# A hybrid decoder block on one core: GpSimd subtracts 1,024 columns in four instructions of 256

## The chip, the cores and the metric

The kernel runs on one core of a Trainium2 chip. The metric is the device time of one execution in microseconds, as the median of several runs. The engines are called PE (TensorE's matmuls; PEld are its weight loads), DVE (VectorE), ACT (ScalarE), POOL (GpSimd) and SP (SyncE, which here issues the loads).

## What is computed

One layer of a decoder block on x of 256 tokens by 1,024 channels, in f32. The reference, cut to what matters:

```python
mod = (c @ w_ada + b_ada)                       # 6 x 1024: shifts, scales, gates
h = rms_norm(x, norm_mix) * (1 + sc_m) + sh_m
q_a, kv_a, gl_a, qkv_b, a_b, b_b, z_b, merge = split(h @ w_in)
y_a = nsa_attention(q_a, kv_a, gl_a, ...)       # 16 heads, three branches
y_b = gated_deltanet(qkv_b, a_b, b_b, z_b, ...) # 8 heads, chunked delta rule
mixed = g_a * (y_a @ w_proj_nsa) + g_b * (y_b @ w_proj_gdn)
x = x + gt_m * (mixed @ w_out)
h = rms_norm(x, norm_ffn) * (1 + sc_f) + sh_f
u = causal_depthwise_conv(h @ ffn_up, ffn_conv) + ffn_conv_b
x = x + gt_f * ((silu(u_gate) * u_val) @ ffn_down)
return rms_norm(x, norm_final)
```

## The kernel before

Nearly all the work is matrix products with weights that are read from HBM once, some 118 MB. Each product is done to more than the precision of one pass: a weight w is split into hi, w rounded to the matmul's input type, and lo = w - hi, the activations likewise, and each block of the product is three matmuls: hi times hi, hi times the activation's lo, and lo times the activation's hi (`lin`, lines 255 to 271).

A weight comes in pieces of 128 partitions by 1,024 columns (512 KB). `rawload` (229) asks SP for the load into a ring of five raw buffers, tag `wraw`. `split` (234) then makes hi with a copy on ACT (243) and lo with a subtraction on POOL or DVE (244). The raw buffer is free again when both have read it. hi lies in one of five buffers and lo in one of four, and they are free when TensorE has read them. The down-projection's pieces have buffers of their own (dhi, dlo). Who subtracts is counted out: every second piece goes to POOL in the opening, all of them from line 353 on, and three of five from line 755 on (`pool_share`). In `lin` a piece of 1,024 columns is four blocks of 256, one for each k of 128 input channels, and the matmuls of a block read its 256 columns of hi and lo; one piece feeds 2 x 4 x 3 = 24 matmuls.

The same five raw buffers carry the columns of w_ada (48 pieces, tag `wada`). They take no part in matmuls: DVE multiplies a piece with a broadcast c and sums it up (`adasum`, line 214), which gives 128 entries of mod. In the opening (lines 344 to 349) each of the eight k needs two such sums, then the scaled activation `mt` (298), its hi on ACT (306) and its lo on DVE (307), and two weight pieces of the projection `wko`, one subtracted by DVE and one by POOL.

The order of the opening up to line 341 is written by hand. From there on a planner, which keeps its own times for every instruction, orders the instructions of each engine's queue; the loads on SP stand in one queue, in which a load that waits for its buffer holds up those behind it. `recent` remembers the last instruction on an engine, and some later instructions are put behind it (lines 758, 1069 to 1075).

POOL has other work besides: the low half of the queries (line 884), 64 partitions by 256 columns, one of the weightings of the attention's probabilities (922), a mask (552) and the scaling of keys (524). The lines of DVE that the text names are 465 to 468, small steps of the gates with 16 or 32 columns, and 214 and 244. In the feed-forward part DVE does the taps of the convolution (1114) with one operand in PSUM.

Of the kernel before, what the change touches and what calls it, by code (L numbers as in the profile page):

```python
# [11 lines left out]
F32 = mybir.dt.float32  # L12
# [4 lines left out]
ALU = mybir.AluOpType  # L17
# [5 lines left out]
D = 1024  # L23
# [78 lines left out]
def build(tc, a, probe=None):  # L102
    nc = tc.nc
    V, S, G, TE = nc.vector, nc.scalar, nc.gpsimd, nc.tensor
    with ExitStack() as ctx:
# [17 lines left out]
        def tl(name, tag, shape=None, dt=F32):  # L123
            n, w = TAGS[tag]
            return wk.tile(list(shape or (P, w)), dt, name=name, tag=tag, bufs=n)
# [100 lines left out]
        recent = {}  # L226
# [7 lines left out]
        def split(w, down=False):  # L234
            if down:
                hi, lo = tl("dhi", "dh", dt=F32R), tl("dlo", "dh", dt=F32R)
            else:
                hi = wp.tile([P, D], F32R, name="whi", tag="whi", bufs=5)
                lo = wp.tile([P, D], F32R, name="wlo", tag="wlo", bufs=4)
            cnt[0] += 1  # L240
            n, m = pool_share[0]
            e = G if cnt[0] * n // m != (cnt[0] - 1) * n // m else V
            recent[S] = S.copy(hi, w).ins  # L243
            recent[e] = e.tensor_tensor(lo, w, hi.bitcast(F32), op=ALU.subtract).ins  # L244
            return hi, lo

        def loadw(src, down=False):

            return [split(rawload(src[i]), down) for i in range(src.shape[0])]
# [87 lines left out]
        t = scaled(0)  # L337
        shifted(0, t, V)
        ko(0, 0, *split(wko[0]))
        ko(0, 1, *split(wko[1]))  # L340
        start.close()

# [93 lines left out]
        w = wp.tile([P, D], F32, name="wraw", tag="wraw", bufs=NRAW)  # L436
        nc.sync.dma_start(out=w[:, :512], in_=a["wg"])
        w = w[:, :512].rearrange("p (k c) -> p k c", k=KB)
# [100 lines left out]
        for h in range(NH):  # L539
            for c in range(2):  # L540
# [5 lines left out]
                e = tl("e", "tg")  # L546
# [8 lines left out]
                            op=ALU.add, negate=True)  # L555
# [55 lines left out]
        n = range(2)  # L611
# [523 lines left out]
        for f in range(NF):  # L1135
# [8 lines left out]
            t, w = o  # L1144
# [31 lines left out]
        for k in range(KB):  # L1176
            (G if k in POOLK else V).tensor_tensor(x2b[k], x2b[k], r, op=ALU.mult)
            if k in OUTS:
                lo = OUTS[k]
# [66 lines left out]
```

## Time and profile before

| what | us |
|---|---|
| runs | 655.29, 654.51, 653.84 |
| median | 654.51 |
| profiled execution, device time | 651.43 |
| its span, first to last instruction | 649.4 |
| busy: PE, DVE, ACT, POOL | 583.3, 512.1, 381.5, 342.1 |

The profile is of one execution. A row of a group gives the number of instructions, their busy time in all, the mean of one in ns, and the idle time of the engine just ahead of them with what ended it. An instruction that stands still after its start, for whatever reason, counts as busy. The chain is found from the last instruction back, at each step to what released it or to the instruction before it on its engine. Matmuls are pipelined, so that their durations overlap. Spans on POOL are rough.

### The profile page before, as it was taken

To read this page: it belongs to the slowest core of one execution; us is meant where nothing else is said; L and a number is where in the kernel's file an instruction comes from. 1 tells how busy PE (TensorE), PEld (TensorE's weight loads), DVE (VectorE), ACT (ScalarE), POOL (GpSimd) and SP (SyncE) were. 2 spreads that over 40 slices of the span, in tenths; PEclk is the share of its full clock that TensorE was granted. 3 is DMA by queue.
4 is the path that set the end of the run, shared out by engine and by line. 5 is a ranking of instruction groups with operands and counts; after the bars stand their busy time and mean duration, and the time that the engine had idled before them with its cause. 6 is when DMAs were issued, how large, how long until landed. Compare 5 with 4: busy or idle time off the path is not lost.

```text
span 649.4 us, 13709 instructions
## 1 busy us (share of the span) xinstructions
PE 583.3 (90%) x5128; PEld 550.4 (85%) x5128; DVE 512.1 (79%) x1206; ACT 381.5 (59%) x858; POOL 342.1 (53%) x239
## 2 busy tenths in 40 slices
PE   7888999899988888999898998698599999999794
PEld 4787998788988886999776998698599999989793
DVE  5999869789999998697967789697966576766845
ACT  4335988645565686596776633376765545435554
POOL 3324897735666877365631435265474545435531
PEclk9999999999998899899999999799699999999998
DMA  7789665344675744234414456864557456566401
GB/s 293 272 288 338 207 210 191 110 153 133 225 257 203 245 147 147 83 98 132 147 49 164 136 183 207 318 224 134 184 180 246 168 195 229 195 223 230 165 1 65
DMA packets 35364, 119.73 MB, mean 184 GB/s; under 512 B 4961, under 2 KB 5729, under 8 KB 35298
## 3 DMA queue, kind: packets, MB, share of 16 engines
q1 hardware_dynamic: 35298, 118.86, 53.6%
q8 instruction: 40, 0.66, 0.4%
q14 instruction: 26, 0.21, 0.1%
HBM read 117.66 MB, written 1.18 MB: 183 GB/s over the span
## 4 chain that ended last, share of the span: by engine, by line
PE 40%; DVE 35%; DMA 10%; ACT 7%; issue 6%; POOL 1%; SPq 0%; DVEq 0%; ACTq 0%; POOLq 0%
PE lin L266 8%; PE lin L268 8%; PE lin L269 8%; DMA wada<-in_ada 8%; DVE wlo L244 7%; DVE wada L214 6%; DVE pp L922 2%; PE dn L1132 2%; PE dn L1131 2%; PE dn L1130 2%; PE y L968 1%; ACT whi L243 1%; DVE cacc L398 1%; DMA wraw<-in_down 1%; DVE tb L577 1%
## 5 line engine op out<-in xcount | busy, mean ns | idle before, releaser
L244 POOL TENSOR_TENSOR wlo<-wraw,whi 128x1024 fp32r<-128x1024 f32 x90 | 228.8, 2551 | 165.3 <-ACT whi L243 97.4
L243 ACT CAST whi<-wraw 128x1024 fp32r<-128x1024 f32 x144 | 150.0, 1048 | 67.9 <-PE lin L268 20.9
L266 PE MATMUL lin<-hh,whi 128*128 128x256 f32 x384 | 111.2, 290 | 1.1 <-DVE cacc L398 0.7
L268 PE MATMUL lin<-hl,whi 128*128 128x256 f32 x384 | 110.7, 289 | 0.0
L269 PE MATMUL lin<-hh,wlo 128*128 128x256 f32 x384 | 110.5, 289 | 0.0
L214 DVE CUSTOM_DVE_ANT_0 wada<-wada,cb,col 128x1024 f32<-128x1024 f32 x48 | 86.1, 1795 | 22.2 <-DMA wada<-in_ada 22.0
L266 PE MATMUL lin<-fh,whi 128*128 128x256 f32 x304 | 85.6, 282 | 8.8 <-DVE up L1148 8.8
L269 PE MATMUL lin<-fh,wlo 128*128 128x256 f32 x304 | 86.0, 283 | 5.7 <-DVE wlo L244 3.9
L244 DVE TENSOR_TENSOR wlo<-wraw,whi 128x1024 fp32r<-128x1024 f32 x54 | 88.1, 1632 | 2.8 <-ACT whi L243 2.2
L268 PE MATMUL lin<-fl,whi 128*128 128x256 f32 x304 | 85.5, 281 | 0.0
L266 PEld LDWEIGHTS lin<-hh,whi 128*128 128x128 f32 x384 | 74.1, 193 | 2.0 <-ACT whi L243 0.9
L269 PEld LDWEIGHTS lin<-hh,wlo 128*128 128x128 f32 x384 | 74.1, 193 | 0.8 <-issue 0.3
L268 PEld LDWEIGHTS lin<-hl,whi 128*128 128x128 f32 x384 | 74.0, 193 | 0.6
L266 PEld LDWEIGHTS lin<-fh,whi 128*128 128x128 f32 x304 | 58.3, 192 | 9.0 <-ACT fh L1103 9.0
L269 PEld LDWEIGHTS lin<-fh,wlo 128*128 128x128 f32 x304 | 58.3, 192 | 7.0 <-DVE wlo L244 5.0
L244 POOL TENSOR_TENSOR dlo<-wraw,dhi 128x1024 fp32r<-128x1024 f32 x14 | 37.4, 2676 | 49.8 <-ACT dhi L243 48.4
L268 PEld LDWEIGHTS lin<-fl,whi 128*128 128x128 f32 x304 | 58.4, 192 | 0.0
L1132 PE MATMUL dn<-ah,dlo 128*128 128x256 f32 x176 | 48.8, 277 | 0.6 <-POOL dlo L244 0.6
L1131 PE MATMUL dn<-al,dhi 128*128 128x256 f32 x176 | 48.6, 276 | 0.0
L1130 PE MATMUL dn<-ah,dhi 128*128 128x256 f32 x176 | 48.6, 276 | 0.0
L915 ACT ACTIVATE pp<-pp,misc 128x128 f32<-128x128 f32 x64 | 28.4, 446 | 13.5 <-DVE misc L907 13.4
L1132 PEld LDWEIGHTS dn<-ah,dlo 128*128 128x128 f32 x176 | 33.1, 188 | 1.0 <-POOL dlo L244 1.0
(410 smaller groups left out, 1597.7 us busy)
## 6 DMA issues: line engine op xcount, KB each, us to landing
wraw<-in_win SPq DMA_DIRECT2D x52, 512.0 KB, 3.6
wada<-in_ada SPq DMA_DIRECT2D x48, 512.0 KB, 3.9
wraw<-in_up SPq DMA_DIRECT2D x44, 512.0 KB, 4.2
wraw<-in_down SPq DMA_DIRECT2D x22, 512.0 KB, 3.8
wraw<-in_wko SPq DMA_DIRECT2D x16, 512.0 KB, 5.2
wraw<-in_pn SPq DMA_DIRECT2D x8, 512.0 KB, 3.5
wraw<-in_pg SPq DMA_DIRECT2D x8, 512.0 KB, 3.5
wraw<-in_wo SPq DMA_DIRECT2D x8, 512.0 KB, 3.9
```

Source lines behind the costliest of these rows:

```text
L214: V.tensor_tensor_reduce(w, w, cb, 1.0, cl("bada", m), ALU.mult, ALU.add, mod[:, m:m + 1])
L243: recent[S] = S.copy(hi, w).ins
L244: recent[e] = e.tensor_tensor(lo, w, hi.bitcast(F32), op=ALU.subtract).ins
L266: TE.matmul(o[:, b], hi[:, j, cs], hh[k], start=k == 0 and b == 0, stop=False, skip_group_check=True)
L268: TE.matmul(o[:, b], hi[:, j, cs], hl[k], start=False, stop=False, skip_group_check=True)
L269: TE.matmul(o[:, b], lo[:, j, cs], hh[k], start=False, stop=k == KB - 1 and b == blocks - 1, skip_group_check=True)
L398: V.scalar_tensor_tensor(acc[:, sft:], src[:, :T - sft], col[:, w0 + 3 - sft:w0 + 4 - sft], acc[:, sft:], op0=ALU.mult, op1=ALU.add)
L915: S.activation(pv, pv, AF.Exp, bias=mx[:, 1 + w, t, r:r + 1], accum_out=sm[:, 1 + w, t, r:r + 1])
L922: (G if 2 * w + t in POOLP else V).tensor_scalar(pv, pv, wt[:, 1 + w, t, r:r + 1], None, op0=ALU.mult)
L1130: TE.matmul(o, hi[:, cs], ah, start=f == 0 and b % 2 == 0, stop=False, skip_group_check=True)
L1131: TE.matmul(o, hi[:, cs], al, start=False, stop=False, skip_group_check=True)
L1132: TE.matmul(o, lo[:, cs], ah, start=False, stop=f == NF - 1 and b % 2 == 1, skip_group_check=True)
```

## The change

Where POOL does a subtraction, it does so in four instructions of 256 columns each, one behind the other; where DVE does, the instruction stays one of 1,024. `recent` then holds the fourth.

```diff
             recent[S] = S.copy(hi, w).ins
-            recent[e] = e.tensor_tensor(lo, w, hi.bitcast(F32), op=ALU.subtract).ins
+
+            n = 4 if e is G else 1
+            for i in range(n):
+                c = slice(D // n * i, D // n * (i + 1))
+                recent[e] = e.tensor_tensor(lo[:, c], w[:, c], hi[:, c].bitcast(F32), op=ALU.subtract).ins
             return hi, lo
```

## Rows read from the trace of the kernel before

**Rows 1.** The page's busy times: engine, us, share of the span, instructions.
```profile
PE 583.3 (90%) x5128; PEld 550.4 (85%) x5128; DVE 512.1 (79%) x1206; ACT 381.5 (59%) x858; POOL 342.1 (53%) x239
```

**Rows 2.** The page's chain that ended last, shares of the span by engine.
```profile
PE 40%; DVE 35%; DMA 10%; ACT 7%; issue 6%; POOL 1%; SPq 0%; DVEq 0%; ACTq 0%; POOLq 0%
```

**Rows 3.** Line 244 alone: ns of one, min/median/max; first and last start in us.
```profile
L244 POOL TENSOR_TENSOR wlo<-wraw,whi x90: 2345/2406/3484, 14.2 to 604.9; 128x1024 fp32r<-128x1024 f32 x90
L244 DVE TENSOR_TENSOR wlo<-wraw,whi x54: 1191/1219/3403, 14.5 to 609.5; 128x1024 fp32r<-128x1024 f32 x54
L244 POOL TENSOR_TENSOR dlo<-wraw,dhi x14: 2402/2409/3397, 461.9 to 628.6; 128x1024 fp32r<-128x1024 f32 x14
```

**Rows 4.** Groups of DVE by form, and line 214 alone (min/median/max).
```profile
L244 DVE TENSOR_TENSOR wlo<-wraw,whi 128x1024 fp32r<-128x1024 f32 x54 | 88.1, 1632 | 2.8 <-ACT whi L243 2.2 <-PE lin L269 0.3 <-ACT zt L751 0.2
L214 DVE CUSTOM_DVE_ANT_0 wada<-wada,cb,col 128x1024 f32<-128x1024 f32 x48 | 86.1, 1795 | 22.2 <-DMA wada<-in_ada 22.0
...
L214 DVE CUSTOM_DVE_ANT_0 wada<-wada,cb,col x48: 1235/1285/3448, 9.2 to 585.4; 128x1024 f32<-128x1024 f32 x48
```

**Rows 5.** Timeline of DVE, 50 to 56 us: start, us, instruction, idle before.
```profile
50.78 3.25 DVE L214 CUSTOM_DVE_ANT_0 wada<-wada,cb,col 128x1024 f32<-128x1024 f32 x1 [0.31 <-DMA wada<-in_ada]
```

**Rows 6.** Timeline of POOL, 50 to 56 us.
```profile
50.55 2.40 POOL L244 TENSOR_TENSOR wlo<-wraw,whi 128x1024 fp32r<-128x1024 f32 x1 [4.58 <-ACT whi L243]
```

**Rows 7.** Timeline of DVE, 95 to 103 us.
```profile
95.57 1.55 DVE L465 TENSOR_TENSOR misc<-misc,col 128x16 f32<-128x16 f32 x1
97.04 2.42 DVE L466 TENSOR_SCALAR misc<-misc 128x16 f32<-128x16 f32 x1
```

**Rows 8.** Timeline of POOL, 92 to 103 us (merged), and the last of the four alone.
```profile
89.98 9.45 POOL L244 TENSOR_TENSOR wlo<-wraw,whi 128x1024 fp32r<-128x1024 f32 x4
...
97.05 2.37 POOL L244 TENSOR_TENSOR wlo<-wraw,whi 128x1024 fp32r<-128x1024 f32 x1
```

**Rows 9.** Timeline of DVE and of POOL, 221 to 233 us.
```profile
221.69 1.33 DVE L214 CUSTOM_DVE_ANT_0 wada<-wada,cb,col 128x1024 f32<-128x1024 f32 x1
...
222.02 3.27 POOL L244 TENSOR_TENSOR wlo<-wraw,whi 128x1024 fp32r<-128x1024 f32 x1
```

**Rows 10.** The chain in order of time: start, us, what.
```profile
14.55 3.41 DVE wlo L244
...
47.09 3.67 DMA wada<-in_ada
...
54.07 3.84 DMA wada<-in_ada
...
609.46 2.21 DVE wlo L244
...
626.27 5.73 POOL dlo L244 x2
```

**Rows 11.** Lines 884 and 552 alone on POOL: ns, min/median/max.
```profile
L884 POOL TENSOR_TENSOR qq<-qT,qq x32: 716/733/1695, 84.2 to 324.7; 64x256 fp32r<-64x256 f32 x32
...
L552 POOL TENSOR_TENSOR um<-U,cst x8: 625/628/1606, 130.7 to 167.3; 128x256 f32<-128x256 f32 x8
```

**Rows 12.** Windows: us, busy PE, PEld, DVE, ACT, POOL; then line 244's DVE, POOL.
```profile
72.00:135.00 63.00, 59.37 (x486) 56.50 (x485) 50.30 (x126) 49.60 (x148) 49.22 (x34) 1.00 0.52 170
465.00:600.00 135.00, 133.25 (x1151) 132.59 (x1150) 89.04 (x136) 71.03 (x111) 68.87 (x27) 0.99 0.60 206
...
72.00:135.00 63.00, 2.54 (x2) 39.95 (x17) 1.00 0.52 170
```

**Rows 13.** SP's own waits: line, waited for whom, us in total, times, longest.
```profile
SPq L231 <- POOL wlo L244: 107.8, 45, 5.3
...
SPq L210 <- POOL wlo L244: 28.8, 7, 7.5
```

## The prediction, made before the changed kernel was run

> **What bounds the kernel now.** I began with the busy times. TensorE's matmuls fill 90% of the span, VectorE (DVE) 79%, GpSimd (POOL) 53% [rows 1]. The chain that ended last names another culprit beside TensorE: 40% of the span lies on PE, 35% on DVE, 10% on transfers, 1% on POOL [rows 2]. So POOL, the engine that the change touches, sets the end almost nowhere by itself; the reader is to ask what it does to DVE.
>
> The spread of one instruction answers that. Line L244 on DVE takes 1.219 us at the median and 3.403 at most; on POOL 2.406 and 3.484 [rows 3]. The groups of DVE have means far above the clean time: L244 1632 ns against 1219, the adaLN sum of L214 1795 against its median of 1285 [rows 4]. That is 54 x 0.41 = 22 us and 48 x 0.51 = 24 us of waiting inside the instructions. The timeline shows why. The adaLN sum that starts at 50.78 meets a POOL subtraction which began at 50.55 and runs 2.40; it ends at 54.03, 1.08 us after POOL [rows 5, 6]. A DVE instruction that works within SBUF stands still until the whole POOL instruction is over. It is no matter of length: L466, one operand of 16 columns, took 2.42 us beside a POOL subtraction of 2.37 [rows 7, 8]. It goes the other way too: a POOL subtraction that starts while the sum at 221.69 runs takes 3.27 us [rows 9].
>
> How much of it lies on the chain? From the piece at 14.55 (3.41 us) to the one at 609.46 (2.21), 23 of its pieces are L244 or L214 stretched beyond 1.22 and 1.29 us; their excess sums to 33 us [rows 10]. Short instructions such as L465 and L466 (1.55 and 2.42 us for 16 columns) [rows 7] add some 20 more by the same count, an estimate. So about **53 us of 649** is DVE on the chain, waiting for POOL.
>
> **The change, part by part.** All subtractions keep their engine; 90 + 14 = 104 POOL instructions of 1,024 columns [rows 3] become 416 of 256.
>
> *Price of a piece.* The trace holds no such piece. The nearest rows are L884, the same operation over 256 columns on 64 partitions, 0.733 us at the median, and L552, 256 columns on 128 partitions with a multiply, 0.628 [rows 11]. POOL's neighbours in a row overlap by some 0.03 us: four subtractions from 89.98 took 9.45 us, 2.36 each [rows 8]. Four pieces then last 4 x 0.628 - 3 x 0.03 = 2.42 to 4 x 0.733 - 0.09 = 2.84 us, against 2.41. I take 2.84, the row of the same operation: **+0.43 us each, 45 us of POOL in all**, 342 to 387 of 649. The lower end is +0.01, 1 us in all.
>
> *Where POOL's extra lies.* Mostly beside idle time. The critical stretch is 72 to 135 us, where every subtraction goes to POOL: 49.2 of 63 us busy, PE 59.4 [rows 12]. One POOL subtraction feeds 24 matmuls, and TensorE, at 1151 matmuls in 135 us [rows 12], passes 24 in 2.8 us: POOL at 2.84 just keeps up, but its lead shrinks. Seventeen subtractions there cost 7 us, more than half of 13.8 us of POOL idle. If that cover is gone TensorE waits for all 7 or 8 us. Against it stands that the first piece is there after 0.73 us where the whole came after 2.41, and matmuls that read one block of the weight can begin on it. I take +2 us, bounds 0 and +8. At the end two subtractions in a row (626.27, 5.73 us) stand on the chain [rows 10]; the last piece comes 0.9 later, but TensorE starts on earlier pieces: 0, bounds -2 and +1.
>
> *What DVE gets back.* An instruction that waits now waits for a piece, not for the rest of 2.40 us. Since the sum at 50.78 ended 1.08 us after POOL and needs 1.285 alone, 0.2 of a wait is covered; a piece costs at most 0.73 - 0.20 = 0.53. But POOL is back in the queue after every piece, so a second DVE instruction of this kind can meet the second piece: four waits of 0.53 are 2.1, and one whole wait today is 2.40 - 0.20 = 2.2. Where DVE runs such instructions without a pause, **the total stays as it is**. That is the case at 14 to 72 us. Its round runs from one load of a column block of `ada` to the next, 47.09 to 54.07 [rows 10]: the load takes 3.67, then the sum at 50.78 takes 3.25 and frees the buffer for the next load. That sum would end 1.7 us earlier, and the load behind it would go out earlier; but the second sum, mt and wlo then meet the other three pieces. The round's 6.98 us hold 0.31 in which DVE waits for the load and 3.25 - 1.29 = 1.96 in which it waits for POOL [rows 5]; the 4.71 that are left, plus 2.12, are 6.83. Some 12 of the 53 us lie in this stretch, and I book 0, bounds -1 (six rounds of 0.15) and +8 (the third rival's).
>
> Elsewhere 53 - 12 = 41 us remain. The 23 pieces waited 1.4 us on average; two waits of about 0.35 in place of it halve them: **-20 us** on this chain. What is late next: TensorE, full at 465 to 600 us (133.25 of 135) [rows 12], and the ring of raw buffers with transfers of 3.7 us and more [rows 10]. I give half to them: **-10**, bounds 0 and -20.
>
> *Waits that the change adds.* None is written, but SP sends the next load when POOL's last piece has released its raw buffer; SP stood on POOL 45 + 7 times, 107.8 + 28.8 us, with all later loads queued behind [rows 13]. ACT's casts wait for those loads. This price is the third rival's.
>
> *Order of the queues.* Outside the opening the planner orders the work by its own times of each instruction, and four short ones are other entries than one long. No row prices that; I bound it by one ring transfer of 3.8 us [rows 10] either way, taken as 0.
>
> Sum: -10 + 2 = **-8 us**. The profiled execution took 651.43 us (span 649.4), so 643.4 there; it lies 3.1 under the median of 654.51, and against that the time is **646.5**.
>
> **A rule that speaks against it.** The Trainium skill (SBUF — State Buffer, section Who interferes with whom) says that the shared port pair is held for a whole instruction, and that issue order decides which side blocks. [Rows 9] agree that POOL can be the blocked side. By that rule each piece is a new turn in which POOL may be the one to wait, and the time is the third rival's 662 us; by the idle time of POOL in [rows 1] it is 646.5.
>
> **Rivals.** *Larger gain.* Nearly all 41 us leave the chain and half of that shows: -20 + 2 = -18, 636.5 us. For it: PE waits stand behind DVE's. Against: PE 90% busy. Chance 0.13.
>
> *Hidden.* DVE's waits shrink, but the next chain, PE with its buffers, is as long; within 1.3 us of 654.5. Chance 0.10.
>
> *POOL hands the buffers back late (slower).* Where DVE is dense, each piece waits for a 1.2 us instruction, and a subtraction takes 4 x (0.53 + 1.2) = 6.9 us instead of 2.41 to 3.48. A raw buffer is free 0.4 to 3.4 us later, say 1.5; over 52 waits of SP that is 78 us of later issue, and with 10% of the span's chain on transfers, +8: 662 us. It decides once more than half of the pieces wait for DVE. For it: [rows 13]. Against: POOL idles 47%. Chance 0.22.
>
> *The pieces do not let DVE in.* Then the edit does not do what it says: 53 us of waits grow by 0.43/2.40, 9.5 us, half of it shown, +5: 659 us. Against it: L465 (95.57, 1.55) ended at 97.12, although the next POOL subtraction had already begun at 97.05 [rows 7, 8]; so DVE got its turn between neighbours. The Trainium skill (GPSIMD Engine Reference, section Instruction dispatch) says that a core starts the next instruction when its own share is done, without waiting for the other cores; by that rule no instant need be free between pieces. Chance 0.05.
>
> **How the numbers follow.** My forecast has 0.47, with a range of its own of 640 to 652. A further 0.03 for a planner's order that costs time. Faster 0.47 + 0.13 = 0.60, no difference (within 0.2%, which is about what a measurement of this kernel can tell) 0.10, slower 0.22 + 0.05 + 0.03 = 0.30. The range reaches from below the larger gain, 634, to the ring's 662.
>
> **What would show it.** Right: L244 on POOL 416 times near 0.73 us; L214's mean nearer 1.4 than 1.8 us and no DVE instruction of 16 columns above 0.8; DVE's share of the chain well under 35%. Wrong in the step of halving: L214 and L244 on DVE still average over 1.6 us. Wrong by the ring: SP's wait for POOL far above 137 us, TensorE waiting for POOL's wlo. Wrong by price: pieces above 0.8 us when nothing holds them, POOL above 70% of the span.

## The result and the profile after

The changed kernel took **633.35 us** (median of four runs, 628.62 to 635.48) against 654.17 of the kernel before (four runs, 650.24 to 655.29): a ratio of 0.9682, 95% interval 0.9614 to 0.975, 20.8 us less. The forecast was 646.5 with a range of 634 to 662: the sign was right, the time lies just below the range, and the gain was more than twice the forecast one. The profiled execution after took 628.62 us with a span of 626.8; it is the fastest of the four, 4.7 below their median, so between the two profiles 22.6 us of span are to be explained. The lines of the code have moved by four (244 is now 248). In three of the later kernels one run each took over 1.5% longer than the fastest of the same kernel; it is left out of their times.

The page's busy times and the shares of the chain, which answer to [rows 1, 2]:

```profile
PE 579.2 (92%) x5128; PEld 546.3 (87%) x5128; DVE 468.0 (75%) x1206; ACT 382.5 (61%) x858; POOL 431.5 (69%) x551
...
PE 53%; DVE 17%; DMA 10%; ACT 7%; POOL 7%; issue 3%; SPq 1%; DVEq 0%; ACTq 0%; POOLq 0%
```

DVE lost 44 us of busy time with the same 1,206 instructions, POOL gained 89. On the chain DVE went from 35% of 649 us (227) to 17% of 627 (107); PE went from 40% to 53% and POOL from 1% to 7%. Span minus PE's busy time is 66.1 us before and 47.6 after: 18.5 of the 22.6 us are time in which TensorE had nothing to do, 4.1 are its matmuls themselves.

Line 248 alone (ns, min/median/max), the two DVE groups with their means, and line 214 alone, which answer to [rows 3, 4]:

```profile
L248 POOL TENSOR_TENSOR wlo<-wraw,whi x360: 718/738/1792, 14.5 to 588.4; 128x256 fp32r<-128x256 f32 x180
L248 POOL TENSOR_TENSOR dlo<-wraw,dhi x56: 723/740/1797, 446.6 to 607.7; 128x256 fp32r<-128x256 f32 x56
L248 DVE TENSOR_TENSOR wlo<-wraw,whi x54: 1206/1240/1765, 14.6 to 585.7; 128x1024 fp32r<-128x1024 f32 x54
...
L248 DVE TENSOR_TENSOR wlo<-wraw,whi 128x1024 fp32r<-128x1024 f32 x54 | 74.4, 1377 | 4.7 <-ACT whi L243 3.9 <-PE lin L273 0.7
L214 DVE CUSTOM_DVE_ANT_0 wada<-wada,cb,col 128x1024 f32<-128x1024 f32 x48 | 70.4, 1470 | 29.6 <-DMA wada<-in_ada 29.4
...
L214 DVE CUSTOM_DVE_ANT_0 wada<-wada,cb,col x48: 1270/1384/1871, 9.7 to 562.7; 128x1024 f32<-128x1024 f32 x48
```

The longest DVE subtraction for `wlo` is 1.77 us where it was 3.40; the means fell from 1632 to 1377 and from 1795 to 1470 ns. The starts on POOL tell where the time was gained, as far as the new order leaves the same work in the same place. Beside those of `dlo` above, the low halves of the queries (line 884, now 888) answer to [rows 11]:

```profile
L888 POOL TENSOR_TENSOR qq<-qT,qq x32: 717/734/1753, 85.6 to 318.4; 64x256 fp32r<-64x256 f32 x32
```

The first low half of the queries starts at 85.6 us where it was 84.2, so the opening gained nothing that shows there; the last starts 6 us earlier (318.4 against 324.7), the first `dlo` 15 us (446.6 against 461.9) and the last 21 us (607.7 against 628.6). Behind the opening the gain is spread over the kernel.

What was one wait is now several short ones. The timelines of DVE and of POOL at 50 us [rows 5, 6], then of DVE at 94 us [rows 7]:

```profile
50.16 1.81 DVE L214 CUSTOM_DVE_ANT_0 wada<-wada,cb,col 128x1024 f32<-128x1024 f32 x1 [0.83 <-DMA wada<-in_ada]
...
52.16 1.49 DVE L214 CUSTOM_DVE_ANT_0 wada<-wada,cb,col 128x1024 f32<-128x1024 f32 x1
...
50.16 4.97 POOL L248 TENSOR_TENSOR wlo<-wraw,whi 128x256 fp32r<-128x256 f32 x4 [2.30 <-ACT whi L243]
...
94.61 0.48 DVE L469 TENSOR_TENSOR misc<-misc,col 128x16 f32<-128x16 f32 x1
95.01 0.78 DVE L470 TENSOR_SCALAR misc<-misc 128x16 f32<-128x16 f32 x1
```

The sum that took 3.25 us takes 1.81, and the 16-column step that took 2.42 takes 0.78. POOL pays: its four pieces between DVE's instructions took 4.97 us. By themselves they cost what was forecast, as POOL's timeline at 577 us shows, with POOL's groups (the two groups stood at 228.8 and 37.4 us before):

```profile
577.63 2.83 POOL L248 TENSOR_TENSOR dlo<-wraw,dhi 128x256 fp32r<-128x256 f32 x4 [2.59 <-ACT dhi L243]
...
L248 POOL TENSOR_TENSOR wlo<-wraw,whi 128x256 fp32r<-128x256 f32 x360 | 307.5, 887 | 105.0 <-ACT whi L243 51.7 <-PE lin L273 22.5 <-issue 20.1
L248 POOL TENSOR_TENSOR dlo<-wraw,dhi 128x256 fp32r<-128x256 f32 x56 | 46.7, 868 | 32.8 <-ACT dhi L243 23.0 <-issue 9.8
```

Four pieces in 2.83 us, where 2.84 had been taken. The groups sum to 354.2 us, 88 more than 266.2: 45 are the price of the pieces, and the other 43 are longer waits for DVE, an estimate from these sums.

The windows of [rows 12], SP's waits of [rows 13] and TensorE's waits for POOL's low halves:

```profile
72.00:135.00 63.00, 60.43 (x495) 56.96 (x494) 48.19 (x132) 52.07 (x152) 59.03 (x85) 1.00 0.52 164
465.00:600.00 135.00, 133.25 (x1161) 132.45 (x1160) 83.02 (x140) 73.37 (x114) 93.25 (x108) 1.00 0.63 207
...
SPq L231 <- POOL wlo L248: 123.0, 61, 5.5
SPq L210 <- POOL wlo L248: 53.9, 15, 8.9
...
PE ko L318 <- POOL wlo L248: 2.3, 5, 0.9
PE lin L273 <- POOL wlo L248: 1.6, 2, 1.1
```

At 72 to 135 us POOL is now busy 59.0 of 63, with 4.0 idle where 13.8 were; yet TensorE passes 495 matmuls there instead of 486. SP stands on POOL for 177 us instead of 137, and TensorE waits 3.9 us in all for these pieces, where it waited 3.3 for POOL's whole subtractions.

### The profile page after: what moved, and what is told of

It is laid out like the page before. It is cut to its first block, busy times and chain, and to the rows that moved or that the text cites. A ratio compares the mean times of both kernels' runs of the same rounds, so it can differ in the third digit from the quotient of the medians.

```text
span 626.8 us, 14062 instructions
## 1 busy us (share of the span) xinstructions
PE 579.2 (92%) x5128; PEld 546.3 (87%) x5128; DVE 468.0 (75%) x1206; ACT 382.5 (61%) x858; POOL 431.5 (69%) x551
## 4 chain that ended last, share of the span: by engine, by line
PE 53%; DVE 17%; DMA 10%; ACT 7%; POOL 7%; issue 3%; SPq 1%; DVEq 0%; ACTq 0%; POOLq 0%
PE lin L270 11%; PE lin L273 11%; PE lin L272 11%; DMA wada<-in_ada 6%; POOL wlo L248 5%; PE dn L1135 3%; PE dn L1136 3%; PE dn L1134 3%; DVE wada L214 3%; ACT whi L243 2%; DVE wlo L248 2%; DMA wraw<-in_wko 2%; DVE pp L926 2%; PE y L972 1%; DMA wraw<-in_win 1%
## 5 line engine op out<-in xcount | busy, mean ns | idle before, releaser
L248 POOL TENSOR_TENSOR wlo<-wraw,whi 128x256 fp32r<-128x256 f32 x360 | 307.5, 887 | 105.0 <-ACT whi L243 51.7
L270 PE MATMUL lin<-hh,whi 128*128 128x256 f32 x384 | 109.7, 286 | 1.1 <-DVE cacc L402 1.1
L272 PE MATMUL lin<-hl,whi 128*128 128x256 f32 x384 | 109.1, 285 | 0.0
L270 PE MATMUL lin<-fh,whi 128*128 128x256 f32 x304 | 85.6, 282 | 8.7 <-DVE fl L1108 8.7
L214 DVE CUSTOM_DVE_ANT_0 wada<-wada,cb,col 128x1024 f32<-128x1024 f32 x48 | 70.4, 1470 | 29.6 <-DMA wada<-in_ada 29.4
L248 DVE TENSOR_TENSOR wlo<-wraw,whi 128x1024 fp32r<-128x1024 f32 x54 | 74.4, 1377 | 4.7 <-ACT whi L243 3.9
L273 PEld LDWEIGHTS lin<-hh,wlo 128*128 128x128 f32 x384 | 72.8, 190 | 1.7 <-POOL wlo L248 1.0
L248 POOL TENSOR_TENSOR dlo<-wraw,dhi 128x256 fp32r<-128x256 f32 x56 | 46.7, 868 | 32.8 <-ACT dhi L243 23.0
L318 PE MATMUL ko<-hh,wlo 128*128 128x256 f32 x128 | 32.7, 289 | 2.8 <-POOL wlo L248 2.3
```

The lines of the kernel that those rows point to most:

```text
L214: V.tensor_tensor_reduce(w, w, cb, 1.0, cl("bada", m), ALU.mult, ALU.add, mod[:, m:m + 1])
L248: recent[e] = e.tensor_tensor(lo[:, c], w[:, c], hi[:, c].bitcast(F32), op=ALU.subtract).ins
L270: TE.matmul(o[:, b], hi[:, j, cs], hh[k], start=k == 0 and b == 0, stop=False, skip_group_check=True)
L272: TE.matmul(o[:, b], hi[:, j, cs], hl[k], start=False, stop=False, skip_group_check=True)
L273: TE.matmul(o[:, b], lo[:, j, cs], hh[k], start=False, stop=k == KB - 1 and b == blocks - 1, skip_group_check=True)
L318: TE.matmul(kob[4 * w + b // 2][:, b % 2], m[:, b * P:b * P + P], h[k], start=k == 0 and i == 0 and b % 2 == 0, stop=k == KB - 1 and i == ...
```

## The experiments

Three things can carry the gain. **Hold**: a POOL instruction holds up DVE for a quarter of the time. **Order**: the planner sees four entries instead of one and orders all queues anew. **Early word**: each piece tells TensorE that it is there, so that the first matmuls need not wait for the fourth. The runs take them apart. All kernels compute the whole reference; each ratio is to the kernel before, run on the same chip in between, with its 95% interval. Where the order is to be kept, the list of instructions is rewritten after the planner is done.

### The hold alone: the old order, pieces told at the fourth

```diff
+def in_pieces(n):
...
+            for j in range(n):
+                s = mybir.SyncInfo(on_wait=list(i.sync_info.on_wait) if j == 0 else [],
+                                   on_update=list(i.sync_info.on_update) if j == n - 1 else [])
+                out.append(mybir.InstTensorTensor(
...
+    regroup(nc, in_pieces(4))
```

> Every queue as before; only, after planning, each POOL subtraction is four instructions of 256 columns, and whoever waits for it waits for the fourth. Theory A (DVE waits for a quarter of a subtraction): 633 to 640 us, the line of the subtraction and the adaLN sum on DVE near 1.4 us on average. Theory B (the planner's new order of the queues makes the gain): 652 to 660. Theory C (TensorE begins on the first quarter): no gain either, 652 or more, since nothing is told before the fourth.

Measured: 645.33 us (643.53 to 648.27), ratio 0.9875 (0.9837 to 0.9913). Its busy times, chain, DVE's sums, and TensorE's waits for the low halves (lines as before the change):

```profile
PE 582.5 (91%) x5128; PEld 552.6 (86%) x5128; DVE 469.7 (73%) x1206; ACT 382.0 (60%) x858; POOL 425.9 (66%) x551
PE 44%; DVE 15%; DMA 15%; POOL 13%; ACT 7%; issue 5%; SPq 1%; DVEq 0%; POOLq 0%; ACTq 0%
...
L214 DVE CUSTOM_DVE_ANT_0 wada<-wada,cb,col 128x1024 f32<-128x1024 f32 x48 | 69.4, 1448 | 38.4 <-DMA wada<-in_ada 35.8
...
PE ko L314 <- POOL wlo L244: 8.0, 6, 2.8
PE lin L269 <- POOL wlo L244: 7.4, 4, 3.5
```

DVE gets back just what it does in the changed kernel (469.7 us busy against 468.0, the sums at 1448 ns against 1470), but the time falls by 8 us only (653.1 for the kernel before in these runs); all three ranges that had been expected miss it. DVE's share of the chain is 15% where it was 35%, and POOL (13%, was 1%) and transfers (15%, were 10%) have grown. The chain in order of time shows how, in the feed-forward part:

```profile
506.38 2.14 POOL dlo L244 x3
508.52 0.97 POOL wlo L244 x2
509.87 5.21 POOL wlo L244 x6
515.09 4.42 DMA wraw<-in_down
...
598.60 3.79 POOL wlo L244 x4
```

A load waits for a raw buffer that POOL's pieces hand back late, which is the forecast's third rival. In the changed kernel the chain has a single entry of pieces between 435 and 615 us (585.42, 3.77 us); the others lie before that.

### The order alone: the new order, each four joined to one instruction

103 of the 104 groups are joined; of one the pieces don't stand side by side.

```diff
+            take = joined if merge else (lambda ap: ap)
...
+            if merge and not last:
+                continue
...
+    regroup(nc, told_late(True))
```

> The queues as the planner orders them for the four short instructions, but the four joined to one of 1,024 columns where they stand next to one another. A: no gain, 650 to 660, DVE's means back above 1.6 us. B: 633 to 640. C: no gain.

Measured: 648.86 us (648.22 to 649.72), ratio 0.9926 (0.9898 to 0.9953). The chain and DVE's sums:

```profile
DVE 36%; PE 23%; DMA 21%; ACT 11%; issue 6%; POOL 2%; SPq 0%; DVEq 0%; ACTq 0%; POOLq 0%
...
L214 DVE CUSTOM_DVE_ANT_0 wada<-wada,cb,col 128x1024 f32<-128x1024 f32 x48 | 89.8, 1872 | 31.1 <-DMA wada<-in_ada 30.8
```

DVE's waits are back, and with them most of the time; 648.86 lies just below the 650 to 660 of the first theory. The order by itself is worth some 4 us against the same 653.1; hold and order, each alone, make 8 + 4 = 12 of 21.

### The early word taken away, in the new order

```diff
-    regroup(nc, told_late(True))
+    regroup(nc, told_late(False))
```

> The changed kernel with its four short instructions, but the first three tell nobody that they are done; the waits of all others end with the fourth. A: at most 3 us above the changed kernel, 633 to 637. B: the same. C: most of the gain is gone, 645 to 655.

Measured: 640.95 us (634.28 to 643.28), ratio 0.9824 (0.979 to 0.9859). About 8 us more than the changed kernel, with runs 9 us apart, and between the ranges that had been expected. The chain, and TensorE's waits for the low halves, in its fastest run:

```profile
PE 49%; DVE 16%; POOL 12%; ACT 9%; DMA 8%; issue 5%; SPq 1%; DVEq 0%; POOLq 0%; ACTq 0%
...
PE ko L318 <- POOL wlo L248: 10.4, 7, 2.6
PE lin L273 <- POOL wlo L248: 4.0, 4, 1.5
```

14.4 us of waiting where the changed kernel has 3.9. So the early word counts here: it takes back what the late end of the pieces costs TensorE. Told late, POOL has 12% of the chain in the new order too, where the changed kernel has 7%.

Hold and order add up: pieces told late gain 7.8 us in the old order (653.1 to 645.33) and 7.9 in the new one (648.86 to 640.95), and both together make some 12. The other 8 or 9 us come with the early word.

### The early word added, in the old order; and the changed kernel again

Each piece now raises POOL's semaphore, and a matmul waits for the piece of its own block.

```diff
+                    piece = a.offset % D // (D // n) + 1
+                    if piece > g[1]:
...
+                        waits.append(wait(g[2], g[0] + piece if piece < n else g[3]))
...
+    regroup(nc, told_early(4))
```

> Order of the queues as before, four pieces, and now each piece tells TensorE of its own end; matmuls of a block of 256 columns wait for their block's piece alone. If the three parts add up (shorter holds of DVE -8, waits for a quarter -7, planner's order -4): 636 to 640. If the early word helps only in the planner's new order: 643 to 647, as with the wait for the fourth.

> The changed kernel once more, beside the others of this call. All theories: 631 to 636, about 7 us under the 641 that it took with the waits ending at the fourth piece.

Measured: 645.93 us (640.96 to 650.04), ratio 0.988 (0.9842 to 0.9918), and beside it the changed kernel at 631.64 (630.23 to 633.34), ratio 0.9663 (0.9636 to 0.9689). In the old order the early word gains nothing. Its busy times, chain and TensorE's waits (lines one further down), and windows (us, then PE, PEld, DVE, ACT and POOL busy, the granted clock, DMA share, GB/s):

```profile
PE 589.4 (92%) x5128; PEld 557.6 (87%) x5128; DVE 470.2 (73%) x1206; ACT 381.9 (59%) x858; POOL 428.6 (67%) x551
PE 45%; DVE 15%; POOL 14%; DMA 14%; issue 6%; ACT 6%; SPq 0%; DVEq 0%; POOLq 0%; ACTq 0%
...
PE lin L270 <- POOL wlo L245: 3.0, 4, 1.1
PE ko L315 <- POOL wlo L245: 1.6, 3, 0.9
...
550.00:559.00 9.00, 9.00 (x82) 9.00 (x81) 5.81 (x11) 3.53 (x6) 7.90 (x9) 1.00 0.79 264
574.00:580.00 6.00, 6.00 (x32) 6.00 (x32) 3.73 (x6) 2.68 (x5) 2.07 (x3) 0.54 0.84 268
```

TensorE's waits for POOL did fall, from 15.4 to 4.6 us, and its idle time (spans of 641.7 and 643.6, minus busy) from 59.2 to 54.2. But the same 5,128 matmuls took 6.9 us longer: at 574 to 580 us, behind a stretch with gaps, the granted clock was 0.54, near the lower level of 1.2 GHz, and 32 matmuls passed in 6 us where 82 pass in 9 at full clock. And POOL is on the chain as before (14%).

With the early word in both, **the order is worth 14.3 us**: 645.93 against 631.64; told late, it was worth 4.4 (645.33 against 640.95). Between the two profiles with the early word lie 13.7 us of span (643.6 and 629.9): TensorE's idle time makes 6.7 of them (54.2 against 47.5) and slower matmuls 7.0 (589.4 us busy against 582.4, at mean granted clocks of 0.953 and 0.969).

### Half of the early word

The changed kernel with the first three pieces silent in the first 41 of the 104 groups, or in the others.

```diff
+        whole &= set(names[:41])
```

> The changed kernel, in which the first 41 of 104 subtractions (those of the first 205 us) tell only at the fourth piece and the others at each. If the early word pays where POOL works without a pause and TensorE follows close behind it (opening and 72 to 135 us): most of the loss of the late word, 638 to 642. If it pays in the rest: 631 to 634.

```diff
+        whole &= set(names[41:])
```

> The complement: the first 41 subtractions tell at each piece, the other 63 at the fourth. By the first theory 631 to 635; by the second 637 to 642.

Measured: 633.61 us (628.36 to 636.81), ratio 0.9683 (0.9645 to 0.9721), and 634.24 (631.77 to 637.56), ratio 0.9714 (0.9685 to 0.9743). Neither half loses more than some 3 us, and both intervals overlap that of the changed kernel, so neither theory came out. The 8 or 9 us of the whole don't split into places; this stayed open.

### How many pieces

In the old order, two pieces told at the second, and two pieces each told; with the planner two, three (256, 256, 512) and eight.

```diff
+    regroup(nc, in_pieces(2))
```

> Order of before, each POOL subtraction two instructions of 512 columns. A: a DVE instruction waits at most 1.0 instead of 2.2 us, so a good half of the gain of four pieces: 640 to 647. B and C: none, 652 to 656.

```diff
+    regroup(nc, told_early(2))
```

> The same with two pieces of 512 columns that each tell TensorE. Two pieces cost POOL less and took 643 with the late word. If the early word is worth its share for the first half: 637 to 641. If POOL's extra time is what limits four pieces, this one is level with four early pieces or below it.

```diff
-            n = 4 if e is G else 1
+            n = 2 if e is G else 1
```

> The change with two pieces of 512 columns, ordered by the planner. If the parts add up and the order for two pieces is as good as that for four: 632 to 640. If the planner's order for two differs by chance: anything from 632 to 655, with DVE's means near 1.55 us either way.

```diff
+            cuts = (0, 256, 512, 1024) if e is G else (0, 1024)
```

> Three pieces of 256, 256 and 512 columns, ordered by the planner: POOL's extra falls by a third, the early word for the first half stays, DVE's longest wait grows to 1.0 us. If the order for short pieces is better by a rule: 630 to 638, near the changed kernel. If the good order came by chance: 632 to 648.

```diff
-            n = 4 if e is G else 1
+            n = 8 if e is G else 1
```

> Eight pieces of 128 columns, ordered by the planner. DVE's waits fall further (at most 0.25 us), POOL needs about 3.6 us a subtraction and is busy over 80% of the span. If holds are all: 625 to 631. If POOL's own time now counts: 635 to 650, with POOL's share of the chain above 10%.

| pieces | old order, told at the last | old order, each told | planner's order |
|---|---|---|---|
| 2 | 642.73 (ratio 0.9836; 0.9804 to 0.9869) | 640.03 (0.9794; 0.9769 to 0.9819) | 637.72 (0.9738; 0.9702 to 0.9774) |
| 3 | | | 634.74 (0.9721; 0.9697 to 0.9745) |
| 4 | 645.33 | 645.93 | 633.35 and 631.64 |
| 8 | | | 661.2 (1.0125; 1.0102 to 1.0147) |

In the old order two pieces do better than four, clearly so when each is told. They load POOL less (378.7 us busy against 425.9), which is the likely reason and was not tried alone. With the planner three and four are level within their intervals and two are a little slower; but each is a single plan, and plans differ by as much (next section). Eight, in one plan, are 8 us **slower than none**, outside both ranges that had been expected. POOL's pieces, one of TensorE's long waits for them (2.46 us; the longest is 3.4) and what came behind it, in the kernel with eight (groups, timeline of PE, windows):

```profile
PE 598.0 (91%) x5128; PEld 562.3 (85%) x5128; DVE 462.9 (70%) x1206; ACT 382.4 (58%) x858; POOL 498.2 (76%) x967
...
L248 POOL TENSOR_TENSOR wlo<-wraw,whi 128x128 fp32r<-128x128 f32 x720 | 365.8, 545 | 75.7 <-ACT whi L243 41.6 <-issue 11.5 <-DVE misc L728 9.8
...
614.07 0.28 PE L272 MATMUL lin<-fl,whi 128*128 128x256 f32 x1
616.81 0.58 PE L273 MATMUL lin<-fh,wlo 128*128 128x256 f32 x1 [2.46 <-POOL wlo L248]
...
606.00:614.00 8.00, 8.00 (x73) 8.00 (x72) 4.08 (x8) 6.49 (x10) 6.46 (x13) 1.00 0.62 198
616.00:624.00 8.00, 7.19 (x33) 6.85 (x34) 4.67 (x11) 3.12 (x7) 6.99 (x17) 0.57 0.60 223
```

Eight pieces of 0.545 us are 4.4 us for one weight piece, whose 24 matmuls take 2.8. DVE has a little less to wait for (462.9 us against 468.0), but TensorE runs out of low halves: it stops for 2.46 us, and then passes 33 matmuls in 8 us where 73 had passed, at a granted clock of 0.57. Against the changed kernel its idle time (span 658.5 minus busy) is 12.9 us longer, 60.5 against 47.6, and its matmuls take 18.8 us more, at a mean granted clock of 0.950 against 0.974. The longer matmuls are the larger part of the loss.

### Other orders: is it one lucky plan?

The share of subtractions between POOL and DVE from line 755 on is started one or two counts later. That gives other orders, each with whole subtractions and with pieces.

```diff
         pool_share[0] = SHARE
+        cnt[0] += 1
```

> The kernel before with the count at line 755 one higher, so that other subtractions (still three of five) fall to POOL and the planner orders anew. If the planner's order is worth several us by chance: between 645 and 662, away from 653. If not: 651 to 656.

> The changed kernel with the same shift. If the gain of four pieces holds for any order: 16 to 24 us under its partner of whole subtractions. If 12 of the 21 us are chance of the order: 4 to 12 under it, since only the holds of 8 are sure.

```diff
         pool_share[0] = SHARE
+        cnt[0] += 2
```

> The kernel before with the count two higher. As whole_phase1: spread of the orders of whole subtractions.

> The changed kernel with the count two higher. As pieces_phase1: 16 to 24 under whole_phase2 if the gain does not hang on the one order, 4 to 12 if it does.

| order | whole | pieces, planned | difference |
|---|---|---|---|
| as it is | 654.17 | 633.35 | 20.8 |
| one later | 660.89 (ratio 1.012; 1.0073 to 1.0168) | 631.5 (0.9681; 0.9649 to 0.9713) | 29.4 |
| two later | 649.92 (0.9948; 0.9928 to 0.9968) | **622.05** (0.9533; 0.9487 to 0.9579) | 27.9 |

The pieces gain 21 to 29 us in each, more than had been expected, so it is not the luck of one plan, though a plan by itself moves the time of either kind by up to 11 us. The last kernel beats both kernels of this case. Its busy times and chain:

```profile
PE 576.7 (93%) x5128; PEld 545.5 (88%) x5128; DVE 472.5 (76%) x1206; ACT 383.7 (62%) x858; POOL 433.7 (70%) x551
PE 57%; DVE 18%; DMA 8%; ACT 8%; POOL 4%; issue 3%; SPq 1%; DVEq 0%; ACTq 0%; POOLq 0%
```

### Frozen order once more, and DVE's own subtractions in halves

From the best pair: the order of the whole subtractions with four pieces told at the fourth; and pieces on POOL with DVE's subtractions in two of 512.

```diff
         pool_share[0] = SHARE
+        cnt[0] += 2
...
+    regroup(nc, in_pieces(4))
```

> The queues as the planner orders them for whole subtractions with the count two higher; after planning each POOL subtraction is four, told at the fourth. If shorter holds alone are worth 8 us in a fixed order: 640 to 644 against 650. If the 8 us belonged to the one order of before: 646 to 654, or 625 to 636 if here holds are all.

```diff
-            n = 4 if e is G else 1
+            n = 4 if e is G else 2
```

> The fastest kernel so far (four pieces on POOL, count two higher) with DVE's own subtractions in two of 512 columns, so that POOL waits for DVE 0.6 us less and TensorE is told of the first half. If POOL's waits for DVE and TensorE's for DVE's subtractions still count: 615 to 620. If DVE's extra instructions cost as much: 621 to 630.

Measured: 646.78 us (642.77 to 650.15), ratio 0.9895 (0.98 to 0.9991), and 627.39 (624.57 to 631.91), ratio 0.9568 (0.9512 to 0.9624). In this frozen order the hold is worth some 3 us against 649.92, and its runs are wider apart than that; planned anew, the pieces are worth 27.9. The halves on DVE come out 5 us slower than 622.05, though the two intervals overlap. DVE's own halves, with the number of them:

```profile
L248 DVE TENSOR_TENSOR wlo<-wraw,whi 128x512 fp32r<-128x512 f32 x104 | 88.7, 891 | 5.8 <-ACT whi L243 2.4 <-PE lin L273 2.1 <-ACT sq L1047 1.0
```

104 halves of 0.891 us stand for 52 subtractions which, whole, took 1.412 each in the kernel without the halves: 88.7 us against 73.4. POOL gets 9.8 us back (423.9 against 433.7), DVE pays 20.6 (493.1 against 472.5). POOL's holding up DVE was worth breaking; the reverse was of no use in the one plan that was tried.

## Why the prediction was right in kind and wrong in size

**What bounds the kernel: right.** DVE waiting for POOL was a large part of the chain. The tests that the text set came out: 416 pieces at 0.738 and 0.740 us, L214 and L248 on DVE at 1470 and 1377 ns, the step that took 2.42 at 0.78, DVE's share of the chain at 17%. One sentence goes further than its rows, that a DVE instruction within SBUF stands still until POOL's is over. It holds for the instructions that the rows show, but not for all. The subtraction at 222.02 [rows 9] lasts until 225.29, and in the middle of it, in the kernel before, DVE did a reciprocal in 0.16 us:

```profile
224.20 0.16 DVE L916 RECIPROCAL misc<-misc 128x4 f32<-128x4 f32 x1
```

**Price of a piece: right; POOL's total: too low.** Four by themselves cost +0.42 us where +0.43 was taken. POOL's 387 us came out at 431.5, for the 43 us by which the waits for DVE grew were in no term of the sum. In the changed kernel POOL has 7% of the chain, in the old order 13 to 14%.

**POOL's extra, +2 with bounds 0 and +8: right** at four pieces that each tell TensorE: it waits 3.9 us for POOL in all, against 3.3 before. With eight the cover is gone, and the loss is greater than the waits, as the clock falls behind them.

**What DVE gets back, -20, half of it shown: the size came out by luck.** The forecast's own case is the old order with four pieces that each tell TensorE, and that kernel gains 7.9 us (645.93 against 653.87) where the sum had been -8. But two errors cancel in it. DVE got back far more than half of its waits: counted as the prediction counts them, the stretched pieces of L214 and L244 on the chain sum to 3 us in that kernel, where they were 33. And much less than half of that showed. In the other frozen order the hold alone was worth some 3 us.

**The opening, booked as 0: right in time, not in reason.** It ended hardly earlier (the last hl on DVE starts at 63.6 us where it was 64.2), but DVE's total did not stay as it was: from 14 to 65 us the sums of L214 fell from 28.9 to 22.5 us. Over the whole kernel, DVE's waits for the loads of these sums grew from 22.0 to 29.4 us.

**The step that failed** is "Order of the queues", bounded at 3.8 us either way and taken as 0. With pieces that each tell TensorE, as the change has them, the planner's new order is worth 14.3 us: it takes 645.93 to 631.64, about what the forecast lacked. The order alone is no more than 4.2 to 4.4 us of that, with whole subtractions as with pieces told late. The rest comes with the early word, which the sum had only as a set-off against POOL's late end: it is worth 8 or 9 us in the new order and nothing in the old one. TensorE's waits for POOL's pieces fall alike in both (15.4 to 4.6 us in the old order, 14.4 to 3.9 in the new), but only in the new one does the time follow, and only there, with the early word, does POOL's share of the chain go down to 7%. Why the two need each other stays open; which queue's order does it was not tried alone.

**The rivals.** "Larger gain", 636.5 us, had the nearest number, but its reason was the hold alone, and that is not it. "Hidden" and "The pieces do not let DVE in" fell: DVE's waits went, and so did the time. "POOL hands the buffers back late" fell in the changed kernel, though SP's waits for POOL grew from 137 to 177 us: fewer than half of the pieces waited, as their median is the clean 0.738. In the old order with pieces its entries stand on the chain. But long waits of SP are no loss by themselves: the fastest kernel, at 622.05 us, has 214.5 us of them.

The Trainium skill (SBUF — State Buffer, section Who interferes with whom) has the lock held for a whole instruction; the trace agrees, as DVE's longest subtraction for `wlo` fell from 3.40 to 1.77 us with the length of POOL's instruction. The slower time worked out beside that rule, 662 us, did not come with four pieces. The Trainium skill (GPSIMD Engine Reference, section Instruction dispatch) lets a core start the next instruction without waiting for the others, by which no gap for DVE need be free between pieces; the four pieces that took 4.97 us instead of 2.83 show that DVE does get in between.

## What to carry to other kernels

Where one engine's long instructions hold up another engine that is on the chain, cut those: two to four pieces were enough here, and eight, in the one plan tried, lost more in fixed cost and in TensorE's slower matmuls than they gave back. Where a planner orders the queues, price a change of granularity with the plan made anew and with the plan frozen; here most of the gain came only when the plan could move around the pieces and each piece told that it was there; with the plan frozen, POOL and the transfers took the freed engine's place on the chain. Plans that differ by a count in a share differed by some 10 us here, so compare pairs in several of them before a gain is put down to an edit.

## What was not expected of the hardware

A GpSimd subtraction on 128 partitions has a fixed part: 0.459 us at the median for 128 columns, 0.738 for 256, 1.296 for 512 (in the kernel with two pieces) and 2.406 for 1,024. That is 2.2 ns a column (1.947 us for 896 columns) and some 0.18 us besides, an estimate from the first and the last that fits the other two.

A stop of TensorE cost more than its length here. In the kernel with eight pieces the granted clock was 1.00 up to 614 us; after 2.46 us without a matmul it was 0.57 from 616 to 624 us, between the two levels of 1.2 and 2.4 GHz. The same matmuls, 5,128 of them, took 575.8 us of busy time in one kernel with pieces, the one told late, at a mean granted clock of 0.977, and 598.0 in the one with eight, at 0.950.
